# Transposed products of a slice: runs of eight wide and eight narrow ones in place of turns

## The chip, the cores and the metric

The kernel runs on one core of one Trainium2 chip. The metric is the time of one execution on the device, in microseconds: 2259.97 us is the median of three runs of the kernel before (2259.74 to 2261.84). Times inside an execution come from one profiled execution of it.

## What is computed

A trunk of two transformer layers over 256 tokens of 2048 features, all in 32-bit floats. Cut to what matters here:

```
h = x
layer 0: mix = fox_attention(h)            # q, k, v, forget gates: h @ w_in (2048 x 6160); 16 heads; @ w_o
layer 1: mix = nsa_attention(h, kv)        # q, gates: h @ w_in; 16 heads over compressed, selected, window keys; @ w_o
both:    h = layer_norm(ALPHA*h + mix)
         h = layer_norm(ALPHA*h + square(relu(h @ w1)) @ w2)      # 2048 -> 8192 -> 2048
after layer 0: kv = h @ kv_w               # six sets of 512 columns; two are compressed by small MLPs
```

Nearly all arithmetic is products of the 256 tokens with weights that come from memory once.

## The kernel before

**Split products.** Weights and activations are each split into a high part, rounded to the format that TensorE multiplies in one pass, and a low part, the rest. A product is high x high + high x low + low x high. ScalarE makes the high part (line 117, tile `whl` for weights, `act` for activations), VectorE subtracts for the low one (line 118). `wload` fetches half a block of weights (128 x 1024, 512 KB, line 114, on SP's queue) into `raw` (4 buffers) and splits it into `whl` (5 buffers of high and low).

**Two kinds of products.** `xs_part`/`xs_mm` (line 173) keeps activations stationary and streams 512 columns of weights, three products per 128 rows and 128 tokens, into two accumulators that take turns every three products. `ws_many` computes a transposed product: one *slice* is 128 columns of a matrix, x^T comes in 16 blocks of 128 features (`kt`), and per block the weights are stationary. The *wide* product (line 151) takes the high weights against high and low activations together, 512 columns; the *narrow* one (line 152) takes the low weights against the high activations, 256 columns. Both add into one accumulator `acc`, the narrow into its first half. `merge` (lines 182 to 189) adds the two halves at the end. Before, a slice issues wide and narrow in turn, block by block; the last block has the narrow one first, since the wide one ends the accumulation.

**Where slices are.** Queries and keys of layer 0 (32 slices, `project`, one after the other, with steps of earlier heads between them), the first MLP matrix of each layer (four quarters of 16 slices, `mlp`), keys and raw keys and values from layer 0's output (16 slices, `ws_stream` with `use_raw` and `use_k`), and queries of layer 1 (16 slices, each in two halves of 8 blocks with steps of other heads between). That is 192 slices. At three places, the first quarter of each layer's MLP and the raw keys and values, the first three slices are computed together, block by block, in three accumulators, because the layer norm in front delivers the activations piece by piece (its transposes are line 367).

**Order.** Each engine runs its instructions in a fixed order. A scheduling layer sets it from the order of the code and its own model of when operands are there; around layer norms it mixes transposes and products. The diff changes the order of the code in `ws_many` alone.

Of the kernel before, what the change touches and what calls it, by code (L numbers as in the profile page):

```python
# [19 lines left out]
P = 128  # L20
S = 256
# [5 lines left out]
KT = D // P  # L27
# [10 lines left out]
BIG = 1e30  # L38
# [14 lines left out]
def constants():  # L53
    """Identity, triangles, stacked identities and masks: they depend on shapes alone."""
    i = np.arange(P)
    eye = np.eye(P, dtype=np.float32)
    upper = (i[:, None] <= i[None, :]).astype(np.float32)
    causal = np.where(i[None, :] > i[:, None], np.float32(BIG), np.float32(0))

    def stacked(n):  # L60
        a = np.zeros((P, n), np.float32)
        a[np.arange(2 * n), np.arange(2 * n) % n] = 1
        return a

    t = np.arange(S).reshape(2, P)
    d_c = t[:, :, None] - (16 * np.arange(NC) + 31)
    keep = (d_c >= 0).astype(np.float32).transpose(1, 0, 2).reshape(P, 2 * NC)
    cst = [eye, upper, np.ones((P, P), np.float32), np.zeros((P, P), np.float32), causal,
           stacked(60), stacked(48), stacked(16), keep]

    def onehot(*dists):
        """Block k of 32 rows picks the bucket of distance k; row 96 + k says that the key lies ahead."""
        a = np.zeros((99, len(dists[0])), np.float32)
        c = np.arange(len(dists[0]))
        for k, dist in enumerate(dists):
            ok = dist >= 0
            a[NB * k + buckets(dist)[ok], c[ok]] = -1
            a[96 + k, c[~ok]] = 1
        return a

    oh = [onehot(255 - np.arange(384))]
    for tb in range(2):
        oh += [onehot(*(d_c[tb, :, n + k] for k in range(3))) for n in range(0, NC, 3)]
    ahead = np.zeros((99, 3, H), np.float32)
    ahead[[96, 97, 98], [0, 1, 2]] = BIG
    oh.append(ahead.reshape(99, 3 * H))
    return np.ascontiguousarray(np.concatenate(cst, 1)), np.ascontiguousarray(np.concatenate(oh, 1))
# [11 lines left out]
def _trunk(nc, tc, i, out, ctx):  # L99
# [23 lines left out]
    def wload(src, k, pool=wp, bufs=5, pieces=1):  # L123
        """Half k of a block of weights, split."""
        raw = raw_tile()
        w = pool.tile([P, 2, HALF], F32R, tag="whl", name="whl", bufs=bufs)
        n = HALF // pieces
        for s in (slice(a, a + n) for a in range(0, HALF, n)):
            load(raw[:, s], src[k][:, s])
            fill_split(w[:, 0, s], w[:, 1, s], raw[:, s])  # L130
        return w
# [10 lines left out]
    def ws_many(srcs, acts, accs, half=None):  # L142
        """accs = (128 columns of a matrix each)^T @ x^T, over the wide halves of x; half: rows 0-1023 or the rest."""
        for kt in range(KT) if half is None else range(8 * half, 8 * half + 8):
            if kt % 8 == 0:
                ws = [wload(src, kt // 8) for src in srcs]
            a = acts[kt // 4][:, kt % 4]
            s = slice(kt % 8 * P, (kt % 8 + 1) * P)
            last = kt == KT - 1
            for w, acc in zip(ws, accs):  # L150
                wide = lambda: mm(acc, w[:, 0, s], a, start=kt == 0, stop=last)  # L151
                low = lambda: mm(acc[:, :S], w[:, 1, s], a[:, 0, :], start=False, stop=False)  # L152
                if last:
                    low(), wide()
                else:
                    wide(), low()

    def ws_stream(srcs, acts, use, together=1):
        """Each of srcs is one 128-column slice of a matrix; use(j, acc) gets its product, transposed."""
        j = 0  # L160
        while j < len(srcs):
            n = together if j == 0 else 1
            accs = [acc_tile() for _ in range(n)]
            ws_many(srcs[j:j + n], acts, accs)
            for k, acc in enumerate(accs):
                use(j + k, acc)
            j += n
# [7 lines left out]
    def xs_part(src, act, accs, first, last, pieces=1):  # L175
        """accs[t] += (512 columns of x)[tokens t] @ 512 x 512 of a matrix"""
        ws = [wload(src, k, pieces=pieces if k == 0 else 1) for k in range(2)]
        for kt in range(4):
            for t in range(2):
                xs_mm(accs[t], act, kt, t, ws[kt // 2], first and kt == 0, last and kt == 3)  # L180

    def merge(dst, acc, scale=1.0):
        """dst = scale * (the wide product's two halves)"""
        t = sp.tile([P, S], F32, tag="mt", name="mt")
        nc.scalar.activation(t, acc[:, S:], AF.Copy, scale=scale)  # L185
        if scale == 1.0:
            nc.vector.tensor_add(dst, acc[:, :S], t)  # L187
        else:
            nc.vector.scalar_tensor_tensor(dst, acc[:, :S], scale, t, op0=OP.mult, op1=OP.add)

    def narrow(src, n, acts, st, dst):
        """dst[:, tok, :] = x @ (2048 x n) for a small n; returns its last step."""
        raw = wp.tile([P, KT, n], F32, tag="raw", name="nraw", bufs=4)
# [32 lines left out]
    def out_proj(src, acts, first, ln=None, two=False, between=()):  # L226
        """h = (ALPHA h or h) + acts @ W, 512 columns at a time (two: the first 1024 at once).

        between's steps come after the parts. With ln, the last 512 columns are left to what it returns,
        which ends with the layer norm."""  # L230
        between = list(between)
# [36 lines left out]
        def end(late, meanwhile=None):  # L268
            """Tokens 128-255 come behind, so that the norm of the others overlaps with their products."""
            ln.gains(late)  # L270
# [30 lines left out]
    class Norm:  # L301
        """Layer norm of h in place, in pieces of 128 tokens x 512 features, with what use does to a piece."""

# [55 lines left out]
    def transposer(cs):  # L359
        """Puts the pieces into cs, transposed and split, in chunks of 512 features."""  # L360
        def use(t, c):
# [30 lines left out]

    # ---- attention: the steps that both kinds share
    def exp_rows(E, L, m, sums):
# [4 lines left out]

    # ================= layer 0: forgetting attention  # L400
    bfb = cp.tile([P, H], F32, name="bfb")
# [8 lines left out]
    def warm(n, lhs, rhs):  # L410
        """Keeps the tensor engine's clock up while it waits."""
        idle = ps_lg.tile([P, 512], F32, tag="lg", name="idle")
        for k in range(n):
            mm(idle, lhs, rhs, start=True, stop=True)
# [16 lines left out]
    def forget_gates():  # L431
        """Log of the forget gates."""
        f = sp.tile([P, 5, 2, H], F32, name="f", bufs=1)
# [144 lines left out]
    with tc.tile_pool(name="late", bufs=2) as late:  # L578
# [6 lines left out]
        def tables():  # L585
            """Tables of the relative bias, negated, with BIG where a key lies ahead"""
            r_ps = ps_lg.tile([P, 512], F32, tag="lg", name="rps")
# [17 lines left out]

    # ================= layer 1: sparse attention over keys and values of layer 0's output
    with tc.tile_pool(name="np", bufs=2) as np_:
# [4 lines left out]
        gate = np_.tile([P, 2, 3 * H], F32, name="gate", bufs=1)  # L612
        # keys of the two branches and of the compressed blocks, split: per group, high and low parts of
        # [selected 0-127, window 0-127, compressed, selected 128-255, window 128-255]
        kT = np_.tile([P, G, 2, KW], F32R, name="kT", bufs=1)
        kcT = np_.tile([P, G, NC], F32, name="kcT", bufs=1)
        vhl = np_.tile([P, 2, 2, 512], F32R, name="vhl", bufs=1)
        v1 = np_.tile([P, 2, 512], F32, name="v1", bufs=1)
        # compressed values in three bands of rows (high, high, low parts), to meet high, low and high weights
        vc = np_.tile([BAND, G, P], F32R, name="vc", bufs=1)  # L620
# [5 lines left out]
        def bands(t):  # L626
            """The three bands of the columns of t"""
            return bass.AP(tensor=t.tensor, offset=t.offset, ap=[*[list(x) for x in t.ap[:-1]], [32, 3], [1, NC]])
# [46 lines left out]
        def compress(s):  # L675
            """First product of the compression; returns its later steps."""
            acc = acc_tile()
# [180 lines left out]
def laid_out(a):  # L858
    """The inputs in the order in which the kernel reads them."""
    def cols(w):  # L860
        # 128 columns of all rows, in two halves of the rows: [n, half, p, (kt c)]
        k, n = w.shape
        return w.reshape(2, k // P // 2, P, n // P, P).transpose(3, 0, 2, 1, 4).reshape(n // P, 2, P, HALF)

    def rows(w):
        # 512 columns of 512 rows, in two halves of the rows: [n, kc, half, p, (kt c)]
        k, n = w.shape
# [53 lines left out]
```

## Time and profile before

| | |
|---|---|
| median of three runs | 2259.97 us |
| profiled execution, first to last instruction | 2258.3 us |
| TensorE busy, products | 2233.2 us (99%) |
| TensorE, loads of stationary operands (beside products) | 1890.7 us |
| VectorE busy | 1406.5 us (62%) |
| ScalarE busy | 1047.0 us (46%) |
| DMA, mean | 189 GB/s |

The span of the profiled execution is its own time here; what the device adds around it is not in the profile. Busy time of TensorE counts overlapping products from start to modelled end, so a group's mean (401 ns for a wide one) is longer than the distance from one start to the next. Distances are read from the timeline. In its rows the first number is the start, the second the time to the end; a row with a count covers that many, from the first start to the last end.

### The profile page before, as it was taken

What the parts mean: (1) busy time and instruction counts of PE and PEld (TensorE: products, weight loads), DVE (VectorE), ACT (ScalarE), POOL (GpSimd) and SP (SyncE); (2) the same over time, 40 slices, a digit from 0 to 9 for tenths busy, and PEclk for the clock granted to TensorE, in tenths of its full rate; (3) what the DMA queues carried; (4) which work ended last, traced back from release to release, by engine and by line L of the source; (5) the groups of instructions that cost most, each with busy time, mean ns of one, the idle gap of its engine ahead of it and who ended that gap; (6) DMA issues with size and microseconds to landing.
All of it is one profiled execution on the core that took longest, in us unless ns stands there. A gap on an engine that the chain in (4) does not pass through costs nothing.

```text
span 2258.3 us, 30147 instructions
## 1 busy us (share of the span) xinstructions
PE 2233.2 (99%) x11478; PEld 1890.7 (84%) x11478; DVE 1406.5 (62%) x2209; ACT 1047.0 (46%) x1564; POOL 18.5 (1%) x26
## 2 busy tenths in 40 slices
PE   9999999999999999999999999999999999999997
PEld 7888888888888888888788888888888888888885
DVE  6565556764565565565786688667655645655655
ACT  5444444443444444444355567544434434444442
POOL 0000000000000000000000000000000000000001
PEclk9999999999999999999999999999999999999998
DMA  7665557556555555555556744565565566565563
GB/s 252 197 206 180 173 197 243 195 187 191 191 186 192 192 187 191 191 187 190 183 170 211 252 134 133 171 212 177 187 194 188 187 194 189 186 195 188 187 194 113
DMA packets 116829, 427.54 MB, mean 189 GB/s; under 512 B 13179, under 2 KB 13339, under 8 KB 115406
## 3 DMA queue, kind: packets, MB, share of 16 engines
q1 hardware_dynamic: 114734, 419.00, 56.9%
q0 software_dynamic: 1952, 6.63, 1.0%
q8 instruction: 90, 1.47, 0.3%
q14 instruction: 53, 0.43, 0.1%
HBM read 423.45 MB, written 4.24 MB: 189 GB/s over the span
## 4 chain that ended last, share of the span: by engine, by line
PE 97%; DVE 2%; DMA 1%; ACT 0%; issue 0%; SPq 0%; DVEq 0%
PE acc L173 44%; PE acc L151 31%; PE acc L152 16%; PE acc L683 1%; PE pt L367 1%; PE pt L830 1%; PE pt L808 0%; PE lg L766 0%; DMA bc<-c_dram 0%; DVE h L354 0%; PE acc L199 0%; PE pt L831 0%; PE pt L524 0%; PE lg L491 0%; PE lg L762 0%; DVE h L339 0%
## 5 line engine op out<-in xcount | busy, mean ns | idle before, releaser
L118 DVE TENSOR_TENSOR whl<-raw,whl 128x1024 fp32r<-128x1024 f32 (+1 forms) x769 | 937.9, 1223 | 617.9 <-ACT whl L117 608.5
L117 ACT CAST whl<-raw 128x1024 fp32r<-128x1024 f32 (+1 forms) x769 | 804.5, 1049 | 740.4 <-PE acc L173 489.6
L151 PE MATMUL acc<-act,whl 128*128 128x512 f32 x3072 | 1089.5, 401 | 0.0
L173 PE MATMUL acc<-whl,act 128*128 128x512 f32 x4416 | 1011.7, 390 | 1.0 <-DVE whl L118 1.0
L173 PEld LDWEIGHTS acc<-whl,act 128*128 128x128 f32 x4416 | 827.6, 188 | 175.4 <-DVE whl L118 1.8
L152 PE MATMUL acc<-act,whl 128*128 128x256 f32 x3072 | 834.3, 282 | 0.0
L151 PEld LDWEIGHTS acc<-act,whl 128*128 128x128 f32 x3072 | 569.7, 189 | 124.1 <-issue 0.2
L152 PEld LDWEIGHTS acc<-act,whl 128*128 128x128 f32 x3072 | 581.4, 189 | 16.7
L185 ACT ACTIVATE mt<-acc 128x256 f32<-128x256 f32 x192 | 73.3, 382 | 308.6 <-PE acc L151 308.6
L187 DVE TENSOR_TENSOR mu<-acc,mt 128x256 f32<-128x256 f32 x128 | 54.1, 424 | 120.3 <-ACT mt L185 120.3
L385 DVE SCALAR_TENSOR_TENSOR mu<-mu 128x256 f32<-128x256 f32 x128 | 54.2, 425 | 4.2
L117 ACT CAST act<-mu 128x256 fp32r<-128x256 f32 x128 | 52.0, 408 | 4.3 <-DVE mu L385 2.6
L118 DVE TENSOR_TENSOR act<-mu,act 128x256 fp32r<-128x256 f32 x128 | 53.4, 419 | 0.0
L117 ACT CAST act<-pt 128x256 fp32r<-128x256 f32 x80 | 29.5, 372 | 43.8 <-PE pt L367 32.7
L241 DVE TENSOR_TENSOR h<-h,acc 128x512 f32<-128x512 f32 x48 | 30.8, 681 | 13.2 <-PE acc L173 13.2
L118 DVE TENSOR_TENSOR act<-pt,act 128x256 fp32r<-128x256 f32 x80 | 33.0, 419 | 9.2 <-ACT act L117 9.0
L395 ACT ACTIVATE E<-E,sm 128x128 f32<-128x128 f32 (+1 forms) x64 | 29.0, 453 | 7.7 <-DVE sm L398 7.4
L354 DVE SCALAR_TENSOR_TENSOR h<-h,mv,lnb 128x256 f32<-128x256 f32 (+1 forms) x53 | 26.5, 541 | 0.1
L395 ACT ACTIVATE E<-L,sm 128x128 f32<-128x128 f32 (+1 forms) x32 | 14.3, 449 | 25.3 <-DVE sm L398 25.3
L367 PE MATMUL pt<-cst,h 128*128 128x128 f32 x96 | 18.8, 294 | 6.3 <-DVE h L354 6.0
L339 DVE SCALAR_TENSOR_TENSOR h<-h,mv,lng 128x256 f32<-128x256 f32 (+1 forms) x53 | 25.0, 501 | 0.0
L239 DVE SCALAR_TENSOR_TENSOR h<-h,acc 128x512 f32<-128x512 f32 x32 | 20.6, 680 | 4.5 <-PE acc L173 4.5
(173 smaller groups left out, 664.9 us busy)
## 6 DMA issues: line engine op xcount, KB each, us to landing
raw<-in_w SPq DMA_DIRECT2D x512, 512.0 KB, 3.5
raw<-in_fq SPq DMA_DIRECT2D x32, 512.0 KB, 3.6
raw<-in_fk SPq DMA_DIRECT2D x32, 512.0 KB, 3.5
raw<-in_fo SPq DMA_DIRECT2D x32, 512.0 KB, 3.6
raw<-in_kvT SPq DMA_DIRECT2D x32, 512.0 KB, 4.4
raw<-in_nq SPq DMA_DIRECT2D x32, 512.0 KB, 3.6
raw<-in_no SPq DMA_DIRECT2D x32, 512.0 KB, 3.6
raw<-in_fv SPq DMA_DIRECT2D x31, 512.0 KB, 3.5
```

The costliest lines, as they stand in the source:

```text
L117: nc.scalar.copy(hi, src)
L118: nc.vector.tensor_sub(lo, src, hi.bitcast(F32))
L151: wide = lambda: mm(acc, w[:, 0, s], a, start=kt == 0, stop=last)
L152: low = lambda: mm(acc[:, :S], w[:, 1, s], a[:, 0, :], start=False, stop=False)
L173: mm(acc, l, w[:, r, s], start=first and n == 0, stop=last and n == 2)
L185: nc.scalar.activation(t, acc[:, S:], AF.Copy, scale=scale)
L187: nc.vector.tensor_add(dst, acc[:, :S], t)
L241: nc.vector.tensor_add(hcols(t, n), hcols(t, n), acc)
L354: nc.vector.scalar_tensor_tensor(hs, hs, rstd, b, op0=OP.mult, op1=OP.add)
L367: nc.tensor.transpose(tp[:, k * P:(k + 1) * P], h[:, t, f:f + P], eye)
L385: nc.vector.scalar_tensor_tensor(u, u, 0.0, u, op0=OP.max, op1=OP.mult)
L395: nc.scalar.activation(E, L, AF.Exp, bias=m, scale=-1.0, accum_out=sums)
```

## The change

Within a slice the products are issued in runs: for blocks 0 to 7 first the eight wide, then the eight narrow ones; for blocks 8 to 15 first the eight narrow, then the eight wide ones. So between two slices sixteen wide products meet. Where three slices are computed together the runs have four blocks and the order turns from weight to weight; the first blocks begin with the wide ones, which open the accumulation, and the last end with them. Comments are removed elsewhere, so that later lines stand nine lines further down: the wide product is line 158 afterwards, the narrow one 160, `xs_mm` 182.

```diff
-        for kt in range(KT) if half is None else range(8 * half, 8 * half + 8):
-            if kt % 8 == 0:
-                ws = [wload(src, kt // 8) for src in srcs]
-            a = acts[kt // 4][:, kt % 4]
-            s = slice(kt % 8 * P, (kt % 8 + 1) * P)
-            last = kt == KT - 1
-            for w, acc in zip(ws, accs):
-                wide = lambda: mm(acc, w[:, 0, s], a, start=kt == 0, stop=last)
-                low = lambda: mm(acc[:, :S], w[:, 1, s], a[:, 0, :], start=False, stop=False)
-                if last:
-                    low(), wide()
-                else:
-                    wide(), low()
+        step = 8 if len(srcs) == 1 else 4
+        for k0 in range(0, KT, step) if half is None else range(8 * half, 8 * half + 8, step):
+            if k0 % 8 == 0:
+                ws = [wload(src, k0 // 8) for src in srcs]
+            turned = k0 // step % 2
+            for n, (w, acc) in enumerate(zip(ws, accs)):
+                def run(wide):
+                    for kt in range(k0, k0 + step):
+                        a = acts[kt // 4][:, kt % 4]
+                        s = slice(kt % 8 * P, (kt % 8 + 1) * P)
+                        if wide:
+                            mm(acc, w[:, 0, s], a, start=kt == 0, stop=kt == KT - 1)
+                        else:
+                            mm(acc[:, :S], w[:, 1, s], a[:, 0, :], start=False, stop=False)
+                order = (False, True) if (turned + n * (step == 4)) % 2 and k0 else (True, False)
+                if k0 + step == KT:
+                    order = (False, True)
+                for wide in order:
+                    run(wide)
```

On TensorE, at the end of one slice of layer 0 (accumulator `acc_2436`) and the begin of the next (`acc_2503`), with one head's attention steps between, stood before:

```order
L151 MATMUL acc_2436<-act_224,whl_2459 128x512
L152 MATMUL acc_2436<-act_224,whl_2459 128x256
L151 MATMUL acc_2436<-act_224,whl_2459 128x512
L152 MATMUL acc_2436<-act_224,whl_2459 128x256 x2
L151 MATMUL acc_2436<-act_224,whl_2459 128x512
L524 MATMUL pt_2484<-PT_2434,v_2184 128x256
L525 MATMUL pt_2484<-PT_2434,v_2184 128x128
L490 MATMUL lg_2489<-fk_2426,fq_2360 128x128
L491 MATMUL lg_2489<-fk_2426,fq_2360 128x256
L151 MATMUL acc_2503<-act_101,whl_2505 128x512
L152 MATMUL acc_2503<-act_101,whl_2505 128x256
```

and stands now:

```order
L158 MATMUL acc_2436<-act_101,whl_2438 128x512 x4
L158 MATMUL acc_2436<-act_146,whl_2438 128x512 x4
L160 MATMUL acc_2436<-act_101,whl_2438 128x256 x4
L160 MATMUL acc_2436<-act_146,whl_2438 128x256 x4
L160 MATMUL acc_2436<-act_185,whl_2459 128x256 x4
L160 MATMUL acc_2436<-act_224,whl_2459 128x256 x4
L158 MATMUL acc_2436<-act_185,whl_2459 128x512 x4
L158 MATMUL acc_2436<-act_224,whl_2459 128x512 x4
L533 MATMUL pt_2484<-PT_2434,v_2184 128x256
L534 MATMUL pt_2484<-PT_2434,v_2184 128x128
L499 MATMUL lg_2489<-fk_2426,fq_2360 128x128
L500 MATMUL lg_2489<-fk_2426,fq_2360 128x256
```

A row with a count is so many in a row; the number behind a tile's name is its buffer's. Where wide and narrow took turns, the narrow products of a slice now stand together, from both halves of its weights, and the wide ones on either side of the attention steps. The attention steps themselves kept their place between the slices.

On TensorE, at the begin of layer 0's MLP (three slices together in `acc_3429`, `acc_3430` and `acc_3431`; `pt` receives the norm's transposes), stood before:

```order
L367 MATMUL pt_3349<-cst_80,h_78 128x128 x4
L151 MATMUL acc_3429<-act_3272,whl_3433 128x512
L152 MATMUL acc_3429<-act_3272,whl_3433 128x256
L151 MATMUL acc_3430<-act_3272,whl_3438 128x512
L152 MATMUL acc_3430<-act_3272,whl_3438 128x256
L151 MATMUL acc_3431<-act_3272,whl_3443 128x512
L152 MATMUL acc_3431<-act_3272,whl_3443 128x256
L151 MATMUL acc_3429<-act_3272,whl_3433 128x512
L152 MATMUL acc_3429<-act_3272,whl_3433 128x256
L151 MATMUL acc_3430<-act_3272,whl_3438 128x512
L152 MATMUL acc_3430<-act_3272,whl_3438 128x256
L151 MATMUL acc_3431<-act_3272,whl_3443 128x512
```

and stands now:

```order
L376 MATMUL pt_3349<-cst_80,h_78 128x128 x4
L158 MATMUL acc_3429<-act_3272,whl_3433 128x512 x2
L158 MATMUL acc_3430<-act_3272,whl_3438 128x512 x2
L158 MATMUL acc_3431<-act_3272,whl_3443 128x512 x2
L158 MATMUL acc_3429<-act_3272,whl_3433 128x512 x2
L160 MATMUL acc_3429<-act_3272,whl_3433 128x256 x2
L376 MATMUL pt_3362<-cst_80,h_78 128x128 x2
L160 MATMUL acc_3429<-act_3272,whl_3433 128x256
L376 MATMUL pt_3362<-cst_80,h_78 128x128 x2
L160 MATMUL acc_3429<-act_3272,whl_3433 128x256
L158 MATMUL acc_3430<-act_3272,whl_3438 128x512 x2
L160 MATMUL acc_3430<-act_3272,whl_3438 128x256 x4
```

The three accumulators now take turns by runs, and the wide products of the first blocks of all three stand before the first narrow one. The transposes for the next piece stand a few products elsewhere.

On SP's queue, at the same place (`w` is the first MLP matrix, `lng` and `lnb` the gains and offsets of the layer norm at that MLP's end), the difference is:

```order
 L114 DMA raw<-in_w 128x1024 x9
 L114 DMA lng<-in_lng 128x2048
-L114 DMA raw<-in_w 128x1024 x3
+L114 DMA raw<-in_w 128x1024 x7
 L114 DMA lnb<-in_lnb 128x2048
-L114 DMA raw<-in_w 128x1024 x244
+L114 DMA raw<-in_w 128x1024 x240
```

The offsets are fetched four weight loads later, here and at the same place of layer 1.

## Rows read from the trace of the kernel before

**Rows 1.** The page: chain that ended last, shares by engine, then by line.
```profile
PE 97%; DVE 2%; DMA 1%; ACT 0%; issue 0%; SPq 0%; DVEq 0%
PE acc L173 44%; PE acc L151 31%; PE acc L152 16%; PE acc L683 1%; PE pt L367 1%; PE pt L830 1%; PE pt L808 0%; PE lg L766 0%; DMA bc<-c_dram 0%; DVE h L354 0%; PE acc L199 0%; PE pt L831 0%; PE pt L524 0%; PE lg L491 0%; PE lg L762 0%; DVE h L339 0%
```

**Rows 2.** The page: groups; busy us, mean ns | idle before.
```profile
L118 DVE TENSOR_TENSOR whl<-raw,whl 128x1024 fp32r<-128x1024 f32 (+1 forms) x769 | 937.9, 1223 | 617.9 <-ACT whl L117 608.5
...
L151 PE MATMUL acc<-act,whl 128*128 128x512 f32 x3072 | 1089.5, 401 | 0.0
...
L152 PE MATMUL acc<-act,whl 128*128 128x256 f32 x3072 | 834.3, 282 | 0.0
...
L152 PEld LDWEIGHTS acc<-act,whl 128*128 128x128 f32 x3072 | 581.4, 189 | 16.7
```

**Rows 3.** Busy time in one stretch: engines, then PEclk, DMA share, GB/s.
```profile
450.00:680.00 230.00, 230.00 (x1192) 196.03 (x1191) 136.31 (x168) 104.61 (x135) 0.00 (x0) 1.00 0.59 189
```

**Rows 4.** Waits: who for whom, us in total, times, longest.
```profile
ACT whl L117 <- PE acc L152: 168.9, 147, 2.3
...
PE acc L173 <- DVE whl L118: 1.0, 2, 0.5
```

**Rows 5.** Chain in order of time, 585 to 690 us: start, us, what.
```profile
592.92 0.47 PE acc L151 x2
...
615.54 0.47 PE acc L151 x2
```

**Rows 6.** Timeline, TensorE, 1002 to 1005 us: start, us, engine, line, tiles, count.
```profile
1002.74 0.40 PE L151 MATMUL acc<-act,whl 128*128 128x512 f32 x1
1002.98 0.28 PE L152 MATMUL acc<-act,whl 128*128 128x256 f32 x1
1003.10 0.40 PE L151 MATMUL acc<-act,whl 128*128 128x512 f32 x1
1003.34 0.28 PE L152 MATMUL acc<-act,whl 128*128 128x256 f32 x1
1003.45 0.40 PE L151 MATMUL acc<-act,whl 128*128 128x512 f32 x1
1003.68 0.28 PE L152 MATMUL acc<-act,whl 128*128 128x256 f32 x1
1003.80 0.40 PE L151 MATMUL acc<-act,whl 128*128 128x512 f32 x1
1004.04 0.40 PE L152 MATMUL acc<-act,whl 128*128 128x256 f32 x2
1004.28 0.63 PE L151 MATMUL acc<-act,whl 128*128 128x512 f32 x2
```

**Rows 7.** Timeline, TensorE, 421 to 431 us.
```profile
421.36 0.39 PE L151 MATMUL acc<-act,whl 128*128 128x512 f32 x1
...
424.82 0.39 PE L151 MATMUL acc<-act,whl 128*128 128x512 f32 x1
...
427.26 0.39 PE L151 MATMUL acc<-act,whl 128*128 128x512 f32 x1
...
430.73 0.39 PE L151 MATMUL acc<-act,whl 128*128 128x512 f32 x1
```

**Rows 8.** Timelines of four runs of wide products, lines 173, 173, 199, 683.
```profile
677.80 4.47 PE L173 MATMUL acc<-whl,act 128*128 128x512 f32 x19
...
2237.61 4.59 PE L173 MATMUL acc<-whl,act 128*128 128x512 f32 x19
...
1174.61 3.89 PE L199 MATMUL acc<-act,nw 128*96 128x512 f32 x16
...
1224.72 4.55 PE L683 MATMUL acc<-whl,winhl 128*120 128x512 f32 x19
```

**Rows 9.** Timeline of a run of three 256-column products.
```profile
1317.82 0.52 PE L830 MATMUL pt<-PT,vhl 128*128 128x256 f32 x3
```

**Rows 10.** Chain in order of time: the 48-column products of line 591.
```profile
399.00 2.38 PE cbps L591 x20
```

## The prediction, made before the changed kernel was run

> **What bounds the kernel now.** I read the chain of waits first: 97% of the chain that ended last is TensorE, and the two lines that the change touches, the wide product (line 151) and the narrow one (line 152), hold 31% and 16% of it [rows 1]. Such a share says nothing of pace, so I went on to the instructions by form: 3072 wide and 3072 narrow products [rows 2], that is 192 slices of 16 pairs. Their recorded 401 and 282 ns are latencies of overlapping instructions, not what one costs. What one costs is the distance from its start to the next start, and that I read from the timeline. Nothing else binds in these stages: in the stretch 450 to 680 us TensorE is busy throughout at full granted clock [rows 3], and the largest wait of TensorE for split weights in the whole run sums to 1.0 us [rows 4]. The other engines wait for TensorE to hand buffers back. So the change is worth what it does to the distances between starts, plus whatever new wait it opens.
>
> **The pace now.** Two slice boundaries of the second quarter of layer 0's MLP, four slices apart, stand at 592.92 and 615.54 us [rows 5]: 22.62 / 4 = 5.655 us a slice, 353.4 ns a pair. The timeline resolves it: from 1002.74 to 1003.80 three pairs pass in 1.06 us, 353.3 ns each; the three wide products take 0.24, 0.24 and 0.23 (mean 236.7 ns), the three narrow ones 0.12, 0.11 and 0.12 (mean 116.7) [rows 6]. Every slice holds one doubled narrow product and borders on a doubled wide one (at 1004.04 and 1004.28), and that leaves its length as the steady pairs give it: 16 x 353.3 = 5653 ns.
>
> But the same instructions also run at another pace. Right behind the first stage start, ten pairs pass from 421.36 to 424.82, 346 ns each (three accumulators taking turns), and ten pairs of an ordinary slice from 427.26 to 430.73, 347 ns each [rows 7]. Same lines, shapes and tiles; soon after it falls to 353.3 and stays there through all four MLP quarters. So the distance between starts is not a property of an instruction; the stream settles into one of several regular patterns. The wide products of line 173 show the same: in the ordinary order 19 of them take 4.47 us, (4.47 - 0.39) / 18 = 226.7 ns, but in the last columns, where the tokens come one after the other, (4.59 - 0.39) / 18 = 233.3 ns [rows 8]. All these paces are whole multiples of 6.67 ns (34, 35, 52 and 53 of them). I use that only as the size of the step by which a pace can be off.
>
> **The change part by part.**
>
> No instruction, byte or shape is added or removed. Moved are 6144 products: within a slice eight wide, sixteen narrow, eight wide, so across slices runs of sixteen of a kind.
>
> *Wide behind wide.* The trace of before has no long run of line 151, but four runs of 512-column products with a new stationary operand nearly each time: 226.7 and 233.3 from above, line 199 (same moving operand as line 151, one accumulator) 16 in 3.89 us, (3.89 - 0.39) / 15 = 233.3, and line 683 (one accumulator) 19 in 4.55 us, (4.55 - 0.40) / 18 = 230.6 [rows 8]. Bounds 226.7 and 233.3. I take 231, their mean. In alternation a wide product costs 236.7, above all four.
>
> *Narrow behind narrow.* The doubled one at each slice's end: 0.40 - 0.28 = 0.12 us [rows 6]. Line 830, three products of 256 columns into one accumulator: (0.52 - 0.28) / 2 = 0.12 us [rows 9]. In alternation 116.7. Bounds 113.3 (one step under 120) and 126.7 (one step over). I take 119, near the rows that are narrow behind narrow.
>
> Pair in the new order: 231 + 119 = 350.0 ns, against 353.3, so 3.3 ns saved.
>
> *How many pairs.* 144 pairs (the first three slices of three stages, which run together) are at 346 to 347 already, 2928 at the slow pace, those of the attention heads taken as slow too: 2928 x 3.33 = 9.8 us saved. The 144 lose 3.3 each: +0.5 us. All of it lies on TensorE, which is the chain.
>
> *Weights.* In the first half of a slice the low parts are now wanted eight wide products (8 x 231 = 1.8 us) later; in the second half both parts are wanted at about the old time. A half's buffer comes back after its sixteenth product as before, so ScalarE's casts, which wait for that [rows 4], come no later. I cost this at nothing; the cover is the slack that lets TensorE wait just 1.0 us for weights now, and if it went, each late half would stop everything by up to the 1.2 us of VectorE's split [rows 2].
>
> *The three stage starts.* With three slices together, four of a kind are issued per weight block, so chunk by chunk of the activations the same products are due; transposes stand at other places among them. On SP the load of the norm's offsets moves behind four more weight loads; it is wanted a whole MLP later. VectorE and ScalarE swap a few splits and merges there. Each start could gain or lose a pair or two of products (2 x 0.353 us); I take 0 and keep plus or minus 2 us for all three.
>
> Sum: -9.8 + 0.5 = -9.3 us. The profiled execution spans 2258.3 us, so 2249.0; the median of the runs shown stands 1.7 us above that span, so 2250.7 us.
>
> The Trainium skill would have it otherwise. In "TensorE: Matmul & The Clock Gate", section "Back-to-back issue gap", the gap of isolated products depends on the number of columns alone (about N/2.4 + 2.5 ns, an estimate of 216 + 109 = 325 ns a pair by that page), whatever stands beside them. By that the order changes nothing. The trace agrees neither with the size (353.3) nor with one pace for one shape (346 and 353 for the same pairs [rows 7, 6]). That the page is right in kind is the first rival below.
>
> **The rivals.**
>
> *No change.* Wide in a run settles at 233.3 as in two of the four rows, narrow at 120 as in both: 353.3, exactly the present pair. For it: wide in one accumulator with the same moving operand is line 199, and its row is 233.3; the doubled pairs of now leave a slice as long as it was. Against it: the present pace is the slowest steady pattern that this trace has for these pairs, and every sixteen products the stream is disturbed anew, which now and then puts it into a faster one. Gain 0, loss 0.5 us at the starts: 2260.5 us.
>
> *Locked fast.* Sixteen wide in a row settle like line 173, at 226.7, with narrow at 120: 346.7, 6.67 x 2928 = 19.5 us, so 2240 us; with narrow at 116.7 it is 29 us, 2231 us. For it: line 173 settles there and stays for 384 products. Against it: there the two accumulators change every three products, and where they don't it runs at 233.3 [rows 8].
>
> *Slower: narrow runs bound by the loads of the stationary operand.* One load is recorded at 189 ns [rows 2], longer than the 120 between narrow products; today every second load lies under a wide product, which gives it back. In runs of sixteen the loads stand in line one per narrow product. From the third or fourth narrow in a row on each would cost one step more, 126.7: 6.67 x 3072 = 20 us less what wide gains, 2270 to 2280 us. At a full load each it would be 69 ns x 3072 = 212 us. Against it: line 830 shows no such growth over three, and twenty 48-column products of line 591 need 2.38 us, 119 ns each, loads included [rows 10]. So the full price is ruled out, one step is not.
>
> **How the numbers follow.** The forecast (pair at 347.5 to 351.8) has 0.45, locked fast 0.17, no change 0.25, slower 0.13. About 0.2% (4.5 us, 1.5 ns a pair) is what a measurement of this kernel can tell from no change. Faster: 0.45 + 0.17 = 0.62; same 0.25; slower 0.13. The range of eight in ten goes from the locked-fast sum with narrow at 120 (2240, its deeper variant left out) to 2264: no change plus the 2 us of the starts and a little of the slower case. The likeliest case's own range is 2243 to 2256.
>
> **What would show it.** Right: a run of sixteen narrow in the timeline at 0.118 to 0.120 each, of sixteen wide at 0.229 to 0.232, an MLP quarter's slice at 5.60 us in place of 5.655, the stage starts within a microsecond of today's, waits of TensorE for split weights still about 1 us. Wrong: slices of 5.65 (no change), wide at 0.227 (locked fast), narrow over 0.123 (slower), or a new wait of TensorE for VectorE's low parts.

## The result and the profile after

The changed kernel takes 2248.1 us (median of four runs, 2247.07 to 2248.97) against 2260.2 us for the kernel before in the same comparison: a ratio of 0.9944, 95% interval 0.993 to 0.9958, so 0.56% faster. The forecast was 2250.7 us and "faster". The profiled execution spans 2246.6 us, 11.7 less than before.

The page of the kernel after: the chain that ended last by engine and by line, and the groups of the changed lines (columns as in [rows 2]).

```profile
PE 95%; DVE 2%; DMA 2%; ACT 0%; issue 0%; SPq 0%; ACTq 0%; DVEq 0%
PE acc L182 44%; PE acc L158 31%; PE acc L160 16%; DMA raw<-in_fq 1%; PE pt L839 1%; PE lg L775 0%; PE pt L817 0%; PE pt L376 0%; DMA raw<-in_fv 0%; DVE whl L118 0%; DMA bc<-c_dram 0%; DVE h L363 0%; PE acc L692 0%; PE pt L840 0%; PE pt L53
...
L158 PE MATMUL acc<-act,whl 128*128 128x512 f32 x3072 | 757.3, 394 | 0.0
...
L160 PE MATMUL acc<-act,whl 128*128 128x256 f32 x3072 | 408.7, 284 | 0.0
```

The shares of the products' lines are those of [rows 1]; TensorE's share in all is 95% for 97%, and DMA has 2% for 1%, with 1% on the load `raw<-in_fq` of weights, which the chain has at the program's begin. The busy times seem to fall by far: 1089.5 and 834.3 us for the wide and narrow products in [rows 2], 757.3 and 408.7 now. The work did not. A product overlaps the next one; in turns wide and narrow were both counted in the overlap, in a run the overlap falls within one group. The means per instruction, 401 to 394 and 282 to 284, say as little. What counts is the distance from start to start, in the timeline of the second quarter of layer 0's MLP (start, us to the last end, line, count):

```profile
594.18 3.82 PE L158 MATMUL acc<-act,whl 128*128 128x512 f32 x16
597.83 2.08 PE L160 MATMUL acc<-act,whl 128*128 128x256 f32 x16
599.75 3.82 PE L158 MATMUL acc<-act,whl 128*128 128x512 f32 x16
603.40 2.08 PE L160 MATMUL acc<-act,whl 128*128 128x256 f32 x16
605.31 2.00 PE L158 MATMUL acc<-act,whl 128*128 128x512 f32 x8
```

A slice is 599.75 - 594.18 = 5.57 us, where [rows 5] gave 5.655. Sixteen wide pass in 3.65 us, 228 ns each against 236.7; sixteen narrow in 1.92, 120 ns each against 116.7 [rows 6]. So wide behind wide gains, and narrow behind narrow loses a little.

Two quarters of an MLP have the same 384 products of line 182 (173 before) between them, so the quarter's period gives the slice more sharply. The chain in order of time, before (start, us, what):

```profile
500.47 87.05 PE acc L173 x384
677.96 87.05 PE acc L173 x384
855.45 87.05 PE acc L173 x384
```

and after:

```profile
498.01 87.04 PE acc L182 x384
674.12 87.04 PE acc L182 x384
850.22 87.04 PE acc L182 x384
```

A period was 177.49 us and is 176.10: (176.10 - 87.04) / 16 = 5.566 us a slice or 347.9 ns a pair, where it was (177.49 - 87.05) / 16 = 5.653 and 353.3. The 384 products themselves take the same 87.04. Laid out by stage, from the start of each stage's first slice in the two traces:

| stretch | after minus before, us |
|---|---|
| program's begin to the first transposed product | +0.98 |
| first four slices of layer 0's heads | +0.60 |
| the other 28 slices of layer 0's heads, to the MLP | -1.88 |
| three slices together: layer 0's MLP, raw keys, layer 1's MLP | -1.12, +1.48, -0.07 |
| the rest of the two MLPs (61 slices each) | -5.19, -5.17 |
| the rest of the keys and values (13 slices) | -0.80 |
| layer 1's heads (16 slices) | -0.45 |
| sum | -11.63 |

The first line holds no changed work; TensorE waits there for the first weights. In the kernels below, which have the same work there, the first transposed product stands anywhere from 1.9 us earlier than after to 0.4 later (33.99 to 36.25 us), a kernel in turns being the latest. So I don't count that line as an effect of the order. The stretches of single slices behind the first four sum to -13.5 us.

The differences at the three starts follow TensorE's granted clock. Busy time of TensorE's products around two of them, layer 0's MLP and the raw keys, before (stretch, its length, busy time and products, granted clock, DMA share, GB/s):

```profile
406.00:409.50 3.50, 3.50 (x13) 0.52 1.01 330
1127.10:1130.60 3.50, 3.50 (x23) 1.00 0.02 5
```

and after:

```profile
405.70:409.20 3.50, 3.50 (x18) 0.80 1.03 336
1120.50:1124.00 3.50, 3.50 (x10) 0.52 0.02 5
```

At a clock near 0.5, the lower level (1.2 GHz), wide products start 427 ns apart by the starts in the trace. Layer 0's MLP had more of it before, the raw keys have it only after, and layer 1's MLP begins with it in both (0.53 and 0.56 over 3.4 and 3.5 us). In front of the raw keys' start TensorE had waited for the norm's pieces in both kernels alike (0.94 and then 0.45 us before, 0.94 and 0.44 after). Kernels below with the same order at that start as after, runs of four and of 32, have 1.00 there, so the fall is not shown to come of the order. Executions of one kernel differ in it too: among 15 of the kernel before, the five at a mean granted clock of 0.997 took 2257.54 to 2259.44 us, the seven at 0.994 or 0.995 2260.21 to 2261.29.

Waits of TensorE after (who for whom: us in total, times, longest), then the timeline around the one new wait:

```profile
ACT whl L117 <- PE acc L160: 164.7, 149, 3.9
...
PE acc L182 <- DVE whl L118: 1.2, 3, 0.5
...
PE acc L182 <- ACT whl L117: 0.8, 1, 0.8
```

```profile
39.73 3.36 PE L158 MATMUL acc<-act,whl 128*128 128x512 f32 x14
43.71 0.40 PE L461 MATMUL pt<-lf,cst 128*128 128x16 f32 x2 [0.62 <-DVE lf L457]
```

ScalarE waits for buffers 164.7 us, where [rows 4] had 168.9. TensorE waits for split weights 1.2 + 0.8 us where it had 1.0; by the timeline the waits of over 0.2 us lie in front of 21 us, at the program's begin. The 0.62 us are the +0.60 of the table. The chain names what came late (start, us, what):

```profile
32.93 3.94 DMA raw<-in_fq
36.94 1.06 ACT whl L117
38.03 1.23 DVE whl L118
39.25 0.10 DVE f L449
```

The forget gates' steps (`f`) stand behind a split of weights on VectorE, and that split behind a load that landed late. VectorE's order there is that of before, when the step of line 449 (then 440) began at 37.25 and TensorE did not wait. Two kernels below with one order of single slices, runs of 32 and the same with turns at the starts, have a wait of 1.18 us at this place and none. So it goes with the loads at the program's begin, and is not shown to be a price of the order.

In the same stretch as [rows 3] TensorE is still busy throughout at full granted clock:

```profile
450.00:680.00 230.00, 230.00 (x1201) 198.18 (x1200) 137.04 (x168) 104.57 (x134) 0.00 (x0) 1.00 0.63 190
```

### The profile page after: what moved, and what is told of

Read it like the earlier page. It is cut to its first block, busy times and chain, and to the rows that moved or that the text cites. A ratio compares the mean times of both kernels' runs of the same rounds, so it can differ in the third digit from the quotient of the medians.

```text
span 2246.6 us, 30144 instructions
## 1 busy us (share of the span) xinstructions
PE 2220.6 (99%) x11478; PEld 1893.7 (84%) x11478; DVE 1408.0 (63%) x2209; ACT 1048.2 (47%) x1564; POOL 18.6 (1%) x26
## 4 chain that ended last, share of the span: by engine, by line
PE 95%; DVE 2%; DMA 2%; ACT 0%; issue 0%; SPq 0%; ACTq 0%; DVEq 0%
PE acc L182 44%; PE acc L158 31%; PE acc L160 16%; DMA raw<-in_fq 1%; PE pt L839 1%; PE lg L775 0%; PE pt L817 0%; PE pt L376 0%; DMA raw<-in_fv 0%; DVE whl L118 0%; DMA bc<-c_dram 0%; DVE h L363 0%; PE acc L692 0%; PE pt L840 0%; PE pt L533 0%; PE lg L771 0%
## 5 line engine op out<-in xcount | busy, mean ns | idle before, releaser
L158 PE MATMUL acc<-act,whl 128*128 128x512 f32 x3072 | 757.3, 394 | 0.0
L158 PEld LDWEIGHTS acc<-act,whl 128*128 128x128 f32 x3072 | 563.5, 189 | 107.3 <-issue 0.2
L160 PEld LDWEIGHTS acc<-act,whl 128*128 128x128 f32 x3072 | 398.2, 191 | 16.9 <-DVE whl L118 0.3
L160 PE MATMUL acc<-act,whl 128*128 128x256 f32 x3072 | 408.7, 284 | 0.0
```

The lines of the kernel that those rows point to most:

```text
L158: mm(acc, w[:, 0, s], a, start=kt == 0, stop=kt == KT - 1)
```

## Experiments

The questions: is the gain one of long runs, or of fewer turns between wide and narrow? What does a turn cost, and why does it cost anything? Where does the gain lie? All ratios are against the kernel before, with 95% intervals; "slice" is the quarter's period less its 384 products, divided by 16.

### Runs of two

```diff
-        step = 8 if len(srcs) == 1 else 4
+        step = 1 if len(srcs) == 1 else 4
```

> Runs of two wide and two narrow where one slice is computed at a time; nothing else changed against the changed kernel. Theory A (settling): a wide product costs 226.7 ns only after about five wide ones in a row, so runs of two gain nothing over turns: a quarter's slice at 5.62 to 5.68 us, whole kernel about 2260 us. Theory B (each change between wide and narrow has a fixed price, the change from turns to runs of sixteen having saved 86.7 ns a slice for 28 fewer changes, 3 ns each): half the changes are gone, slice 5.61 us, whole kernel 2254 us.

2248.22 us, ratio 0.9945 [0.993, 0.9961]: the same as the changed kernel, which neither expectation had. Its timeline:

```profile
600.61 0.62 PE L158 MATMUL acc<-act,whl 128*128 128x512 f32 x2
601.07 0.40 PE L160 MATMUL acc<-act,whl 128*128 128x256 f32 x2
601.31 0.63 PE L158 MATMUL acc<-act,whl 128*128 128x512 f32 x2
601.78 0.39 PE L160 MATMUL acc<-act,whl 128*128 128x256 f32 x2
602.00 0.63 PE L158 MATMUL acc<-act,whl 128*128 128x512 f32 x2
```

Four pairs take 602.00 - 600.61 = 1.39 us, 348 ns a pair. The chain's quarters start at 497.25 and 673.46, so a slice is 5.573 us. Long runs are not needed for the gain.

### Runs of eight

```diff
-        step = 8 if len(srcs) == 1 else 4
+        step = 4 if len(srcs) == 1 else 4
```

> Runs of eight in place of sixteen where one slice is computed at a time. Theory A: each run of eight wide costs 233, 236, 228, 233, 231 and then three times 227 ns (mean 230), narrow 119: slice 5.59 us, whole kernel about 2251 us. Theory B: four changes a slice, 80 of the 86.7 ns saved, slice 5.573 us, whole kernel 2249 us.

2252.13 us, ratio 0.996 [0.9946, 0.9973].

```profile
601.68 2.00 PE L158 MATMUL acc<-act,whl 128*128 128x512 f32 x8
603.52 1.11 PE L160 MATMUL acc<-act,whl 128*128 128x256 f32 x8
604.48 1.78 PE L158 MATMUL acc<-act,whl 128*128 128x512 f32 x7
```

Eight pairs from 601.68 to 604.48 are 2.80 us, and the quarters (498.98, 675.40) give a slice of 5.586. The settling theory had 5.59. By the slice that is slower than runs of two (5.573); the intervals of the two ratios overlap.

### Runs of 32

Two slices at a time, in two accumulators, with the wide ones of both next to each other and then the narrow ones of both.

```diff
+        if len(srcs) == 2:
+            for k0 in (0, 8):
+                ws = [wload(src, k0 // 8) for src in srcs]
+                for wide in ((True, False) if k0 == 0 else (False, True)):
+                    for w, acc in zip(ws, accs):
+                        ...
...
-            n = together if j == 0 else 1
+            n = together if j == 0 and together > 1 else min(2, len(srcs) - j)
```

> Slices of the MLP and of the keys and values computed two at a time, so that thirty-two wide and thirty-two narrow products stand in a row. Theory A: wide settles at 226.7 after five and holds, mean 227.5, narrow 119.8: 5.557 us a slice (5.567 now), whole kernel about 2246.7 us. Theory B: one change a slice in place of two, 3 ns, 5.564 us, 2247.7 us. If fewer buffers ahead make TensorE wait for weights, slower than 2248 instead, with waits for VectorE's split in the trace.

2246.35 us, ratio 0.9936 [0.9923, 0.9948].

```profile
600.69 4.00 PE L158 MATMUL acc<-act,whl 128*128 128x256 f32 x32
604.53 7.44 PE L156 MATMUL acc<-act,whl 128*128 128x512 f32 x32
```

32 narrow take 604.53 - 600.69 = 3.84 us, 120 ns each; the wide ones (7.44 - 0.39) / 31 = 227.4. Quarters (499.08, 675.02): 5.556 us a slice, as the settling theory said. The step from runs of sixteen is small: the interval overlaps that of the changed kernel.

### Turns of equal length

The order of before, but the narrow products as wide as the others, so that they also add low x low.

```diff
-                low = lambda: mm(acc[:, :S], w[:, 1, s], a[:, 0, :], start=False, stop=False)
+                low = lambda: mm(acc, w[:, 1, s], a, start=False, stop=False)
```

> The order of before (turns), but the narrow product is made 512 columns wide too (it also adds low x low). Theory A in the form that unlike lengths keep the stream from settling: all products settle at 226.7 ns, 453.3 a pair, 100 ns x 3072 = 307 us over before, about 2567 us. Rival C (it is the turning between the high and the low weights, or the one accumulator, that keeps it from settling): 233.3 to 236 ns each, 466.7 a pair or more, 2608 us or more.

2568.79 us in one run, beside 2567 expected where the loss comes of unlike lengths, and 2608 by its rival. The timeline:

```profile
699.79 0.39 PE L151 MATMUL acc<-act,whl 128*128 128x512 f32 x1
700.02 0.39 PE L152 MATMUL acc<-act,whl 128*128 128x512 f32 x1
...
700.93 0.61 PE L152 MATMUL acc<-act,whl 128*128 128x512 f32 x2
701.38 0.62 PE L151 MATMUL acc<-act,whl 128*128 128x512 f32 x2
...
702.51 0.39 PE L151 MATMUL acc<-act,whl 128*128 128x512 f32 x1
```

Twelve products from 699.79 to 702.51, 226.7 ns each, in turns and through the doubled pairs. So going from high to low weights and back costs nothing of itself. The loss comes where 512 and 256 columns meet, though not always: the fast pattern of [rows 7] has them in turn too.

### Runs of four

```diff
-        step = 8 if len(srcs) == 1 else 4
+        step = 2 if len(srcs) == 1 else 4
```

> Runs of four where one slice is computed at a time. Theory A' (the floor of a pair is 346.7 ns in any order; every turn from narrow to wide throws the stream out of step, and the price of that depends on the length of the runs: 6.7 ns after runs of one, 3.3 after two, 20 after eight or more): runs of four stand in the changed kernel where three slices go together, and there cost about 15 to 19 ns a turn, so four turns give 5547 + 68 = 5.61 us a slice, more than runs of two (5.573) and of eight (5.587); whole kernel about 2254 us. Theory B' (the longer the run the better, runs of two being a lucky exception or not): between runs of two and eight, 5.57 to 5.59 us, 2248 to 2252 us.

2252.85 us, ratio 0.9968 [0.9956, 0.998].

```profile
600.77 1.09 PE L158 MATMUL acc<-act,whl 128*128 128x512 f32 x4
601.70 0.63 PE L160 MATMUL acc<-act,whl 128*128 128x256 f32 x4
602.17 1.09 PE L158 MATMUL acc<-act,whl 128*128 128x512 f32 x4
603.10 0.64 PE L160 MATMUL acc<-act,whl 128*128 128x256 f32 x4
```

Four wide take 0.93 us, 233 ns each, and four narrow 0.47, 117. Quarters (498.90, 675.77; 87.07 us of line 182) give 5.613 us a slice, the slowest of all runs longer than one. So the time does not fall steadily with the length of the run: runs of two beat four and eight.

### Narrow products of 224 columns

```diff
-                            mm(acc[:, :S], w[:, 1, s], a[:, 0, :], start=False, stop=False)
+                            mm(acc[:, :224], w[:, 1, s], a[:, 0, :224], start=False, stop=False)
```

> The changed kernel with the narrow product cut to 224 columns; the low weights' part is left out for the last 32 tokens. Theory D (every product costs its columns plus 32 clocks, 13.3 ns): narrow in a run at 106.7 in place of 120 ns, 13.3 x 3072 = 41 us less, about 2207 us. Theory E (a narrow product in a run lasts as long as the load of the next stationary operand, 120 ns): narrow stays at 120, whole kernel 2246 to 2250 us.

2243.41 us in one run: neither expectation came. The chain, and a wait of TensorE:

```profile
499.94 87.04 PE acc L182 x384
674.02 87.04 PE acc L182 x384
```

```profile
PE pt L376 <- DVE h L363: 14.4, 18, 2.6
```

The slice fell to (174.08 - 87.04) / 16 = 5.440 us, 340.0 ns a pair: 2.0 us a quarter, some 15 us over both MLPs. Only 5.1 us of it reached the span. TensorE now waits 14.4 us for the layer norm's pieces, 6.0 in the changed kernel; its first quarter, to 499.94, ends 1.9 us later than there (498.01). Shorter products also led to another order around the norms, with fewer products between the transposes, so this run says what 224 columns cost in a settled slice, not what the kernel would gain.

### Turns with 272 columns

```diff
-                low = lambda: mm(acc[:, :S], w[:, 1, s], a[:, 0, :], start=False, stop=False)
+                low = lambda: mm(acc[:, :S + 16], w[:, 1, s], a.rearrange("p k t -> p (k t)")[:, :S + 16], start=False, stop=False)
```

> The order of before (turns) with the narrow product widened to 272 columns (it adds low x low for 16 tokens). Theory E: a product of 272 columns just covers a load, so nothing is pushed on to the wide one, 347 ns a pair, about 2241 us. Theory D: 16 columns more, 6.7 ns a pair: 360 a pair if turns stay in the slow pattern (2281 us), 353.3 if they fall into the fast one (2260 us).

2276.85 us, ratio 1.0076 [1.0057, 1.0094]. Quarters at 505.84 and 684.43, 87.08 us of line 173: 5.72 us a slice, 357.5 ns a pair. Sixteen more columns on every narrow product cost 4.2 ns a pair beside before; the hope that another length would let turns settle in a fast pattern (2241 us) was wrong.

### Turns at the stage starts, runs of 32 elsewhere

```diff
-        step = 8 if len(srcs) == 1 else 4
+        step = 8 if len(srcs) == 1 else 1
...
-                order = (False, True) if (turned + n * (step == 4)) % 2 and k0 else (True, False)
+                order = (False, True) if step > 1 and turned and k0 else (True, False)
```

on top of the kernel with runs of 32; with that step the three slices together take wide and narrow in turn.

> Runs of thirty-two as before in this study, and the three stage starts (three slices together) in turns as in the kernel before. If runs of four cost the starts what they cost elsewhere (about 4 ns a pair over turns there, 144 pairs), 0.5 us under the same kernel without it, 2245.8 us; if the transposes between them decide, within 0.5 us of it either way.

2247.5 us, ratio 0.9944 [0.9932, 0.9957]; with runs at the starts it was 0.9936 [0.9923, 0.9948]. The order at the three stage starts makes no difference that can be told. The traces are sharper than the medians: where the granted clock is 1.00, the raw keys' three slices take 19.32 us in turns, here and before, and 19.26 to 19.32 in three kernels with runs of four; layer 1's MLP's take 19.37 in turns here and 19.16 to 19.18 in runs of four. At half clock either order takes 20.7 to 20.9.

### Turns without the doubled pair

The kernel before without the exchange in the last block: strictly wide, narrow, wide, narrow through all slices.

```diff
-                wide = lambda: mm(acc, w[:, 0, s], a, start=kt == 0, stop=last)
-                low = lambda: mm(acc[:, :S], w[:, 1, s], a[:, 0, :], start=False, stop=False)
-                if last:
-                    low(), wide()
-                else:
-                    wide(), low()
+                wide = lambda: mm(acc, w[:, 0, s], a, start=kt == 0, stop=False)
+                low = lambda: mm(acc[:, :S], w[:, 1, s], a[:, 0, :], start=False, stop=last)
+                wide(), low()
```

> The order of before, but without the exchange in a slice's last block: wide and narrow in turn throughout, no product doubled. Theory F (the stream enters the slow pattern of 353.3 ns a pair when turns begin behind line 173's products and never leaves it by itself): 353.3, about 2260 us. Theory G (it is the doubling at each slice's end that throws it back, and turns alone would keep to the pattern of 346.7 that before shows for some slices): 346.7 in the MLP quarters, 2240 to 2245 us.

2257.26 us, ratio 0.9989 [0.9978, 0.9999]. One timeline, two places: layer 0's first quarter, behind the norm's transposes, and its second, behind line 170 (the wide products of line 173 before):

```profile
439.62 0.39 PE L151 MATMUL acc<-act,whl 128*128 128x512 f32 x1
439.85 0.28 PE L152 MATMUL acc<-act,whl 128*128 128x256 f32 x1
439.97 0.39 PE L151 MATMUL acc<-act,whl 128*128 128x512 f32 x1
...
443.09 0.39 PE L151 MATMUL acc<-act,whl 128*128 128x512 f32 x1
```

```profile
599.74 0.40 PE L151 MATMUL acc<-act,whl 128*128 128x512 f32 x1
599.97 0.28 PE L152 MATMUL acc<-act,whl 128*128 128x256 f32 x1
600.09 0.40 PE L151 MATMUL acc<-act,whl 128*128 128x512 f32 x1
...
602.57 0.40 PE L151 MATMUL acc<-act,whl 128*128 128x512 f32 x1
```

Ten pairs from 439.62 to 443.09 are 347 ns each; eight from 599.74 to 602.57 are 353.8. The whole first quarter keeps the fast pattern, the whole second the slow one, with identical instructions. By the starts in the trace the slow one takes 5653 ns a slice in all six quarters behind line 170, and the fast one 5547 behind each of the three stage starts. Before, the first quarter had the fast one only at its begin [rows 7]: its first single slice took 5561 ns, the next 5651, the others 5653. Without the doubled pairs it stays, so it was they that ended it. Both expectations hold, each at its own places, and the sum is near the first: here the pace goes with how a stretch is entered, and a steady order then keeps it. What it is in the entry that decides is not shown.

### Runs in the MLP alone

The changed order for the MLP's slices, turns everywhere else.

```diff
-        step = 8 if len(srcs) == 1 else 4
+        if not runs_on[0]:
+            step = 1
+        else:
+            step = 8 if len(srcs) == 1 else 4
...
-                order = (False, True) if (turned + n * (step == 4)) % 2 and k0 else (True, False)
+                order = (False, True) if step > 1 and (turned + n * (step == 4)) % 2 and k0 else (True, False)
...
+            runs_on[0] = True
...
+            runs_on[0] = False
```

> Runs as in the changed kernel in the MLP's slices alone; queries, keys and the keys and values in turns as before. By the traces eight quarters gave 1.39 us each at most, some 11 of the 12 us: 2249 us. If the attention slices had carried more than their number says, 2251 to 2255 us.

2250.8 us, ratio 0.9961 [0.9945, 0.9976], so 9.3 of the 12.1 us; its profiled execution spans 2246.5, no more than the changed kernel's, partly because the raw keys' and layer 1's MLP's starts ran at full clock in it (19.4 and 19.2 us, against 20.8 and 20.7 at half clock). Most of the gain lies in the MLPs, and the intervals don't tell how much of the rest does.

### Runs of 32, and of two between the heads

The runs of 32 where slices follow each other, and `step = 1` for single slices.

> Runs of thirty-two in the MLP and in the keys and values, runs of two in the single slices of the two attentions. By the turn prices (3.3 ns for runs of two, 20 for eight or more) the attention slices gain at most 30 ns each over runs of eight and sixteen, 48 x 0.02 = 1 us: 2245.5 us against 2246.4 for runs of thirty-two and 2248.1 for the change.

2245.99 us, ratio 0.994 [0.9928, 0.9953]: no difference from runs of 32 alone that can be told. The quarter's period is that of runs of 32 (497.50 to 673.45). Both kernels are at least as fast as the changed one, by 1.8 and 2.1 us in the medians, within the intervals. In their profiled executions those two starts ran at full clock as well, which is worth some 1.5 us each, so the difference is not shown to come of the order.

## Why the prediction was right, and where its sizes were off

All orders together, with the floor of a pair set to the fast pattern (346.7 ns, 5547 a slice):

| order | slice, ns | turns from narrow to wide | above the floor, ns a turn |
|---|---|---|---|
| in turn, fast | 5547 | 16 | 0 |
| in turn, slow (without the doubled pair; before has 15 turns) | 5653 | 16 | 6.6 |
| runs of 2 | 5573 | 8 | 3.3 |
| runs of 4 | 5613 | 4 | 16.5 |
| runs of 8 | 5586 | 2 | 20 |
| runs of 16 (after) | 5566 | 1 | 19 |
| runs of 32 | 5556 | 1/2 | 18 |

**What bounds the kernel** held: TensorE is the chain, the products of line 182 kept their 87.04 us, and the change is worth what it does to the distances between starts.

**The pair's price** was the step that was mis-sized. 350.0 ns was taken and 347.9 measured, inside the 347.5 to 351.8 of the forecast, but for another reason. Narrow was right, 120 against 119. Wide was taken at 231 as the mean of four rows between 226.7 and 233.3 [rows 8]. It is 228 because a run settles: by the starts in the trace the first five wide products stand 233, 236, 228, 233 and 231 ns apart, the rest 227 or less. So *locked fast* named the right pace for the end of a run, and what keeps the pair from its 346.7 is about 20 ns at each turn: some 28 more over the first five wide products, some 8 less over the first two narrow ones (113 and 119 ns). By the prediction's own signs 0.228 lies below its 0.229 to 0.232, and a slice of 5.57 us below its 5.60. From eight products on that price is constant, so a longer run only thins it out: 5586, 5566, 5556. Against *locked fast* it had been held that line 173 settles only with accumulators that change. The turns of equal length settle in one accumulator for a whole slice of 32 products, so that reason was false.

**How many pairs.** For 122 slices of the MLPs behind the starts the prediction's 3.33 ns gave 122 x 16 x 3.33 = 6.5 us; they gave 10.4 (85 ns a slice). For the 61 slices of heads, keys and values it gave 3.3; the 57 of them behind the first four gave 1.88 + 0.80 + 0.45 = 3.1. In layer 1's heads, where eight wide and eight narrow products stand between attention steps, the gain is least, 0.45 us over 16 slices; eight wide ones behind an attention step stand 235, 233, 236, 224, 231, 236 and 228 ns apart, so such a run ends before it settles. The MLPs gave 3.9 us more than forecast, and the program's begin with the first four slices took back 0.98 + 0.60. That the medians came within 2.6 us of each other is partly luck: the begin has nothing to do with the order, and without it the sum would have missed by more.

**Weights at nothing** held as far as the runs show. TensorE's waits for split weights are 2.0 us for 1.0, all in front of 21 us, and the one new wait of 0.62 us goes with a late load at the program's begin.

**The starts**, +0.5 for lost fast pairs and then 0 plus or minus 2 us: -1.12, +1.48 and -0.07, in sum +0.3. Two of them left the microsecond that the text allowed each, within the 2 us for all three. The prediction weighed transposes and queues there and not the granted clock, which is what they follow: a start that begins at half clock is some 1.5 us longer, in either order. At full clock no fast pairs were lost (19.26 to 19.32 us in runs of four, 19.32 in turns), so the +0.5 does not show.

**The rivals.** *No change* is excluded by the interval, and the reason given for it (the wide at 233.3 in a run) is seen as a mean in runs of four, 0.93 / 4, and not in sixteen. *Slower* is excluded by the rows: narrow stays at 120 through 32 in a row, although loads of the stationary operand stand in line one per product. (The prediction's 119 ns a product for line 591 divides a stretch that takes in the last product's whole time; by their starts they stand 112 apart, which bears it out the more.) The Trainium skill's "Back-to-back issue gap" in "TensorE: Matmul & The Clock Gate" takes the gap of isolated products from the columns alone, and says of a real stream that products and loads together set the spacing; the prediction applied the first to a stream. Here identical products run from 346.7 to 353.3 ns a pair, by their order and by how a stretch was entered, so for this stream the measurement decides against a pace by columns alone.

What stays open: why a turn costs 20 ns behind a run of eight or more and 3.3 behind two, and what sets the pattern that a stretch in turn falls into. The runs show the prices, not their cause.

## What to carry to other kernels

Where TensorE is saturated, read the distance between starts, never the recorded length or the busy share of a line, and compare the same instructions in several places of the trace: two paces for one stretch of code mean that the order is worth an experiment. Put products of one length together, but measure short runs as well as long ones, because the price of a turn is not constant (runs of two beat runs of eight). A gain in products reaches the end only until a layer norm on another engine becomes late (with 224 columns 5.1 of some 15 us reached it), so look at the waits at stage starts after every such gain. Compare the granted clock there too, before a difference at a start is put down to an order: here it was worth 1.5 us, more than the order.

## What the runs showed of the hardware that was not expected

- The same instructions in the same order held two paces for whole stages, 346.7 and 353.3 ns a pair, by what came before the stage. By the starts in the trace the fast one repeats with each pair (230 + 116.7), the slow one with every third: 236 + 113, 232 + 118, 241 + 120.
- The granted clock at a stage start was half for part of it in some kernels and full in others, with the same products and the same wait in front: 20.7 to 20.9 us against 19.2 to 19.4 for three slices of the raw keys or of layer 1's MLP.
- The pace does not fall steadily with the run's length: 5653, 5573, 5613, 5586, 5566, 5556 ns a slice for 1, 2, 4, 8, 16, 32.
- 512-column products in turn with others of 512 run at 226.7 ns throughout, whichever weights they take; in turn with 256 columns they stand at 236.7 on the mean in the slow pattern.
- What repeats steadily repeats after whole multiples of 6.67 ns: a product of a settled run (226.7, 233.3, 120.0), a pair in the fast pattern (346.7), three pairs in the slow one (1060). The prediction's 353.3 is the mean of three unlike pairs, and single distances keep to no such step. 32 columns fewer per narrow product made a pair 7.9 ns shorter than after, 16 columns more 4.2 ns longer than before.
